# Loading group 0's second block of four k-tiles in two lots of two row tiles instead of one lot of four

## Chip, cores, metric

One core of one Trainium2 chip. The metric is device time in microseconds (us) of one execution of the program; a kernel's time is the median of its runs. The experiments ran on four chips, each with runs of the kernel before beside it.

## The reference

```python
def setup_inputs():
    m, k, n = 4096, 4096, 4096
    # a: (m, k), b: (k, n), bias: (n,), all float32, normal
def reference(a, b, bias):
    return np.tanh(np.matmul(a, b) + bias)
```

## The kernel before

8192 matmuls of 128x128 by 128x512 in f16. `a` and `b` are cast from f32 to f16 by the loading DMAs, which GpSimd issues. `a` also has to be turned: a load writes four quarters of 32 partitions (one DMA each), and VectorE transposes 32x32 blocks. The start-up treats eight row tiles of `a` specially: group 0 (`g0`, rows 0 to 3) and group 1 (`g1`, rows 4 to 7), with k in blocks.

```python
P, Q, QP = 128, 4, 32
G, KS, AN, BL, KM = 4, 8, 3, 4, 16

def load_a(m0, nmb, t0, nt):            # nmb x 32 rows, nt k-tiles
    an = anat.tile([P, nmb, nt * QP], fp16, name="an")      # anat: AN = 3 buffers
    for t, n in split(t0, nt):
        for q in (0, 2, 1, 3):
            ...
            nc.gpsimd.dma_start(out=an[ds(q * QP, QP), :, ...], in_=src...)
    return an

def pump():                             # loads in order, at most AN lots alive
    while queue and (queue[0][0] is None or live[0] < AN):
        ...

# order of the loads (cut)
want_a("g1b", G, 4 * P, G * Q, BL, BL)
for i in range(BL):
    want(load_b_next)                   # B tiles, k-tiles 4 to 7
want_a("g0b", G, 0, G * Q, BL, BL)      # "lot B": rows 0-3, k-tiles 4-7
want_a("g0c", G, 0, G * Q, KS, KM - KS) # "lot C": rows 0-3, k-tiles 8-15
for u in range(KS, KM, 2):
    want(lambda u=u: load_b_all(u, 2))  # B in four quarters, two k-tiles each

# TensorE and VectorE (cut)
for m in g0:
    turn(ats[m], "g0b", m * Q, BL, BL)  # transposes of lot B
down(ps, g1, KS - 1, KS, put_aside)
for m in g0:
    turn(ats[m], "g0c", m * Q, KS, KM - KS)
one_by_one(ps, g0, BL, KS, BL)          # 32 matmuls, need lot B
for m in g0:
    across(ps, (m,), KS, KS + 2, BL)    # k-tile 8 on: need lot C and B's quarters
across(ps, g0, KS + 2, KM - 1, BL)
```

The built program allows eight GpSimd DMAs in flight: in its list of waits, each waits for the landing of the one eight places before it. The traces agree: of the 1613 in the trace of before, none was issued before the one eight places earlier had landed, and 241 were issued less than 0.4 us after it.

Of the kernel before, what the change touches and what calls it, by code (L numbers as in the profile page):

```python
# [14 lines left out]
P = 128  # L15
Q = 4
# [7 lines left out]
def kernel(  # L24
# [18 lines left out]
    G = 4  # L43
    KS = 8
    AN = 3
    BL = 4
# [37 lines left out]
    def load_a(m0, nmb, t0, nt):  # L84
        an = anat.tile([P, nmb, nt * QP], fp16, name="an")
        for t, n in split(t0, nt):
            for q in (0, 2, 1, 3):
                k = t * P + q * BL * QP if t < KS else P * KS + (q * (KT - KS) + t - KS) * QP
                src = a[ds(m0, nmb * QP), ds(k, n * QP)]
                nc.gpsimd.dma_start(  # L90
                    out=an[ds(q * QP, QP), :, ds((t - t0) * QP, n * QP)],
                    in_=src.rearrange("(mb p) k -> p mb k", p=QP),
                )
        return an

    def transpose_a(at, an, mb0, t0, nt):

        for t, n in split(t0, nt):
            order = "P mb (k t) -> P mb t k" if t < KS else "P mb (t k) -> P mb t k"
            nc.vector.transpose(  # L100
                at[:, ds(t, n), :].rearrange("P t (mb p) -> P mb t p", p=QP),
                an[:, ds(mb0, Q), ds((t - t0) * QP, n * QP)].rearrange(order, k=QP),
            )
# [11 lines left out]
    def pump():  # L115
        while queue and (queue[0][0] is None or live[0] < AN):
            key, uses, load = queue.pop(0)
            made = load()
            if key is not None:
                live[0] += 1  # L120
                staged[key] = [made, uses]

    def want_a(key, uses, *where):
        queue.append((key, uses, lambda: load_a(*where)))

    def want(load):
        queue.append((None, 0, load))

    def turn(at, key, mb0, t0, nt):
        pump()  # L130
        transpose_a(at, staged[key][0], mb0, t0, nt)
        staged[key][1] -= 1
        if not staged[key][1]:
            live[0] -= 1
            pump()
# [6 lines left out]
    def finish(ps, addend, mi, c0, w=NB, o_sb=None, queues=(nc.sync,)):  # L142
# [22 lines left out]
    ats = [  # L165
        bpool.tile([P, KT, P], fp16, name=f"atx_{m}", tag=f"b_{4 + m}") for m in range(G)
    ] + [atp.tile([P, KT, P], fp16, name="at") for m in range(G)]
# [41 lines left out]
    def down(ps, ms, t0, t1, done):  # L209
        for m in ms:  # L210
            for j in range(J):
                for t in range(t0, t1):
                    mm(ps[m][j], ats[m], b_cur, t, j, False, t == t1 - 1)
                done(ps[m][j], m, j)
# [77 lines left out]
    want_a("g1b", G, 4 * P, G * Q, BL, BL)  # L292
    for i in range(BL):
        want(load_b_next)
    want_a("g0b", G, 0, G * Q, BL, BL)
    want_a("g0c", G, 0, G * Q, KS, KM - KS)
    for u in range(KS, KM, 2):
        want(lambda u=u: load_b_all(u, 2))
# [21 lines left out]
    one_by_one(ps, g1, 0, BL, 0)  # L320
    across(ps, g1, BL, KS - 1, 0)
    for m in g0:
        turn(ats[m], "g0b", m * Q, BL, BL)
    down(ps, g1, KS - 1, KS, put_aside)


# [127 lines left out]
```

## Time and profile before

| kernel before | us |
|---|---|
| median of 3 runs, before the change was made | 1781.98 (1781.78 to 1783.19) |
| median of 6 runs, with the runs beside the changed kernel | 1782.13 (1781.52 to 1783.19) |
| span of the profiled execution | 1780.6 |

The lines are shown in the prediction. They are read in this order: the page's busy row (TensorE works all the time), the chain that ended last in order of time (where the few stops are, and that none comes after 36.44 us), then stretches cut around the stops. Times in the traces count from the first instruction; "landing" is when a DMA's completion is signalled.

### The profile page before, as it was taken

The page shows a single profiled execution, that of the slowest core. Times are in us where ns is not written, and L with a number is a line of the kernel's source. Part 1 is how long each engine was busy: PE and PEld are TensorE (multiplying, and loading weights), DVE is VectorE, ACT ScalarE, POOL GpSimd, SP SyncE. Part 2 cuts the span into 40 slices and gives each one's busy share as a digit, 9 for nine tenths or more (in the row PEclk, how much of TensorE's full clock was granted, in tenths as well). Part 3 has the DMA queues.
Part 4 walks back from the last instruction along what each step waited for, and adds up shares of the span by engine and source line. Part 5 has one row for each costly group of instructions (what it writes and reads, how often), then busy time and mean ns, then how long its engine had stood idle before and what let it go on. Part 6 is the DMA issues. An engine that isn't in the chain of part 4 may idle for free.

```text
span 1780.6 us, 20859 instructions
## 1 busy us (share of the span) xinstructions
PE 1774.4 (100%) x8254; PEld 807.0 (45%) x8254; DVE 763.7 (43%) x682; ACT 172.9 (10%) x281; POOL 872.5 (49%) x1618
## 2 busy tenths in 40 slices
PE   9999999999999999999999999999999999999999
PEld 4444444444444444444444444444444444444444
DVE  3574443444334443444344443444344443444342
ACT  2021000000000000000000000000000000000001
POOL 7465566544565554444456554444544445444510
PEclk9999999999999999999999999999999999999999
DMA  9999999976999877767699997766777667766731
GB/s 183 205 193 177 173 162 166 141 125 110 166 176 164 145 112 116 118 116 120 113 168 173 159 149 116 119 115 109 129 116 121 107 108 121 119 114 109 117 77 42
DMA packets 281393, 238.94 MB, mean 134 GB/s; under 512 B 159056, under 2 KB 231760, under 8 KB 281296
## 3 DMA queue, kind: packets, MB, share of 16 engines
q0 software_dynamic: 243280, 167.88, 69.9%
q1 hardware_dynamic: 37728, 69.62, 11.0%
q8 instruction: 64, 1.05, 0.3%
q14 instruction: 33, 0.27, 0.0%
q10 hardware_dynamic: 288, 0.13, 0.0%
HBM read 337.64 MB, written 67.11 MB: 227 GB/s over the span
## 4 chain that ended last, share of the span: by engine, by line
PE 98%; DMA 1%; POOL 0%; issue 0%; DVE 0%; ACT 0%; POOLq 0%; DVEq 0%
PE ps L415 93%; PE ps L138 5%; DMA an<-in_a_dram 1%; DMA b<-in_b_dram 0%; POOL an L90 0%; POOL nat L246 0%; ACT o_sb L152 0%; DVE atx L100 0%; DVE o_sb L149 0%; POOL b L69 0%; POOL ident L264 0%; POOLq L264 0%; DVEq L149 0%; DVEq L100 0%; POOLq L438 0%
## 5 line engine op out<-in xcount | busy, mean ns | idle before, releaser
L415 PE MATMUL ps<-b,at 128*128 128x512 f16 x7712 | 1657.8, 378 | 0.0
L90 POOL DMA_DIRECT2D an<-in_a_dram x1492 | 805.9, 547 | 797.1 <-DVE at L100 558.6
L415 PEld LDWEIGHTS <-at 128*128 128x128 f16 x7712 | 754.6, 98 | 903.3
L100 DVE STREAM_TRANSPOSE at<-an 128x512 f16<-128x512 f16 (+1 forms) x380 | 565.5, 1539 | 78.2 <-DMA an<-in_a_dram 78.2
L149 DVE TENSOR_TENSOR o_sb<-ps,bias_bc 128x512 f32<-128x512 f32 (+1 forms) x243 | 165.6, 683 | 907.3 <-PE ps L415 697.7
L152 ACT ACTIVATE o_sb<-o_sb 128x512 f32<-128x512 f32 (+1 forms) x243 | 151.4, 624 | 1501.2 <-DVE o_sb L149 1501.2
L73 POOL DMA_DIRECT2D b<-in_b_dram x104 | 56.2, 544 | 14.1 <-DMA an<-in_a_dram 7.0
L138 PE MATMUL ps<-b,atx 128*128 128x512 f16 x256 | 56.2, 379 | 0.6 <-DVE atx L100 0.6
L138 PE MATMUL ps<-b,at 128*128 128x512 f16 x256 | 55.6, 379 | 0.0
L138 PEld LDWEIGHTS <-at 128*128 128x128 f16 x256 | 25.0, 98 | 30.2
L138 PEld LDWEIGHTS <-atx 128*128 128x128 f16 x256 | 24.8, 98 | 30.6 <-DVE atx L100 1.6
L100 DVE STREAM_TRANSPOSE atx<-an 128x512 f16<-128x512 f16 (+2 forms) x12 | 16.3, 1399 | 11.7 <-DMA an<-in_a_dram 11.7
L69 POOL DMA_DIRECT2D b<-in_b_dram x12 | 7.8, 654 | 22.4 <-PE ps L415 22.3
L152 ACT ACTIVATE spill<-spill 128x512 f32<-128x512 f32 x16 | 9.9, 630 | 84.4 <-DVE spill L149 84.4
L149 DVE TENSOR_TENSOR spill<-ps,spill 128x512 f32<-128x512 f32 x16 | 10.2, 674 | 6.2 <-PE ps L138 6.2
L181 DVE TENSOR_TENSOR spill<-spill,bias_bc 128x512 f32<-128x512 f32 x16 | 10.3, 681 | 3.5 <-DMA bias_bc<-in_bias_dram 3.5
L173 ACT COPY spill<-ps 128x512 f32<-128x512 f32 x16 | 8.0, 624 | 12.8 <-PE ps L138 12.8
L228 PE MATMUL ps<-zeros 128*128 128x512 f16 (+1 forms) x14 | 4.7, 504 | 1.3 <-DVE zeros L221 1.3
L176 DVE TENSOR_TENSOR spill<-ps,spill 128x512 f32<-128x512 f32 x8 | 4.8, 674 | 0.0
L228 PEld LDWEIGHTS <-zeros 128*128 128x128 f16 x14 | 1.6, 130 | 3.7 <-issue 2.5
L246 POOL DMA_DIRECT2D nat<-in_a_dram x4 | 2.3, 587 | 0.8 <-POOLq L438 0.8
L239 DVE CAST b<-spill 128x1024 f16<-128x1024 f32 x1 | 0.7, 694 | 4.3 <-DMA spill<-in_b_dram 4.3
(14 smaller groups left out, 9.1 us busy)
## 6 DMA issues: line engine op xcount, KB each, us to landing
an<-in_a_dram POOLq DMA_DIRECT2D x480, 192.0 KB, 5.1
out_dram<-o_sb SPq DMA_DIRECT2D x239, 256.0 KB, 2.7
an<-in_a_dram POOLq DMA_DIRECT2D x960, 32.0 KB, 2.7
b<-in_b_dram POOLq DMA_DIRECT2D x94, 256.0 KB, 8.1
b<-in_b_dram POOLq DMA_DIRECT2D x6, 1024.0 KB, 12.5
an<-in_a_dram POOLq DMA_DIRECT2D x32, 128.0 KB, 5.3
out_dram<-spill SPq DMA_DIRECT2D x16, 256.0 KB, 5.1
an<-in_a_dram POOLq DMA_DIRECT2D x12, 256.0 KB, 8.3
```

What stands on the lines that cost most here:

```text
L69: queue.dma_start(out=dst, in_=src[:, ds(t0 % BL, nt), :])
L73: nc.gpsimd.dma_start(out=bt[t0 // TB][ds(q * QP, QP), ds(t0 % TB, nt), :], in_=src.rearrange("(t p) n -> p t n", p=QP),)
L90: nc.gpsimd.dma_start(out=an[ds(q * QP, QP), :, ds((t - t0) * QP, n * QP)], in_=src.rearrange("(mb p) k -> p mb k", p=QP),)
L100: nc.vector.transpose(at[:, ds(t, n), :].rearrange("P t (mb p) -> P mb t p", p=QP), an[:, ds(mb0, Q), ds((t - t0) * QP, n * QP)].rearrange ...
L138: nc.tensor.matmul(ps, at[:, t, :], bt[t // TB][:, t % TB, ts(j, NB)], start=start, stop=stop)
L149: nc.vector.tensor_tensor(out=o_sb[:, piece], in0=ps[:, piece], in1=addend[:, piece], op=mybir.AluOpType.add)
L152: nc.scalar.activation(o_sb[:, piece], o_sb[:, piece], mybir.ActivationFunctionType.Tanh)
L173: nc.scalar.copy(aside(m, j), ps)
L176: nc.vector.tensor_tensor(out=aside(m, j), in0=ps, in1=aside(m, j), op=mybir.AluOpType.add)
L181: nc.vector.tensor_tensor(out=aside(m, j), in0=aside(m, j), in1=bias_bc[:, ts(j, NB)], op=mybir.AluOpType.add)
L228: nc.tensor.matmul(ps[:, ds(0, w)], zeros[:, :P], zeros[:, :w], start=i == 0, stop=i == n - 1)
L415: nc.tensor.matmul(ps, at[:, t, :], b_cur[t // TB][:, t % TB, ds(c0, w)], start=t == 0, stop=t == KT - 1,)
```

## The change

Intent: TensorE stops before the 32 matmuls that need lot B, and at first they need only row 0. With two lots the transposes of rows 0 and 1 can start when half of lot B has landed.

```diff
-    want_a("g0b", G, 0, G * Q, BL, BL)
+    want_a("g0b", 2, 0, 2 * Q, BL, BL)
+    want_a("g0b2", 2, 2 * P, 2 * Q, BL, BL)
     want_a("g0c", G, 0, G * Q, KS, KM - KS)
...
-        turn(ats[m], "g0b", m * Q, BL, BL)
+        turn(ats[m], "g0b2" if m > 1 else "g0b", m % 2 * Q, BL, BL)
```

## The prediction

> **What bounds the kernel now.** I read the page first: who is busy, the slices, the chain that ended last.
>
> ```profile
> span 1780.6 us, 20859 instructions
> PE 1774.4 (100%) x8254; PEld 807.0 (45%) x8254; DVE 763.7 (43%) x682; ACT 172.9 (10%) x281; POOL 872.5 (49%) x1618
> ...
> PE 98%; DMA 1%; POOL 0%; issue 0%; DVE 0%; ACT 0%; POOLq 0%; DVEq 0%
> ```
>
> TensorE is busy for 1774.4 of 1780.6 us; no transfer change can return more than the 6.2 us in which it is not. The chain in order of time says where those lie:
>
> ```profile
> 19.46 9.00 DMA an<-in_a_dram
> 28.46 0.03 DVEq L100
> 28.49 0.05 issue
> 28.54 0.72 DVE atx L100
> 29.26 0.05 issue
> 29.31 7.08 PE ps L138 x32
> 36.39 0.06 issue
> 36.44 83.04 PE ps L138 x384
> 119.48 1654.20 PE ps L415 x7680
> 1773.68 0.04 DVEq L149
> ```
>
> The piece issued at 19.46 and landing at 28.46 is the fourth DMA of the tile that the change splits (call it lot B: group 0's second block, four row tiles, four DMAs of 128 KB as f16). From 36.44 TensorE never stops again until its last matmul at 1773.68: 83.04 us for 384 matmuls is 0.216 us each, 1654.20 for 7680 is 0.215. So only the time at which TensorE begins at 36.44 matters, and whatever moves that moment moves the end one for one. Two stops lie just ahead of it. I cut the time into stretches around them:
>
> ```profile
> core 0: us, PE busy (x) PEld busy (x) DVE busy (x) ACT busy (x) POOL busy (x), PEclk, DMA share, GB/s
> 14.70:28.60 13.90, 13.90 (x66) 6.17 (x63) 3.30 (x7) 4.10 (x9) 8.65 (x15) 1.00 1.39 177
> 28.60:29.30 0.70, 0.15 (x1) 0.00 (x0) 0.70 (x2) 0.70 (x3) 0.54 (x1) 1.00 1.46 197
> 29.30:36.20 6.90, 6.89 (x32) 3.02 (x32) 4.00 (x5) 1.99 (x5) 3.42 (x7) 1.00 1.22 197
> 36.20:36.45 0.25, 0.20 (x2) 0.04 (x2) 0.25 (x2) 0.00 (x0) 0.25 (x1) 1.00 0.86 156
> ```
>
> Busy time counts a matmul's modelled 379 ns, so the stops look shorter than they are. By starts: matmuls should follow each other by 0.216, and the gaps between starts are 0.936 at 29.31 and 0.434 at 36.44. The first stop thus costs 0.72 us and the second 0.22, 0.94 in all. The first is lot B: its landing at 28.46 is followed by the first transpose at 28.54. For the second the waits name VectorE, but the first transpose of group 0's next lot (lot C, k-tiles 8 to 15) ran from 33.93 for 1.245 us and was over at 35.18. What ended at 36.35 was something else: the matmul of k-tile 8 also needs all four quarters of its B tile, and the fourth was issued at 28.74 and took 7.6 us to land:
>
> ```profile
> L73 POOL DMA_DIRECT2D b<-in_b_dram x1: 535/535/535, 28.7 to 28.7; - x1
> ...
> DMA to landing us min/median/max: 7.6/7.6/7.6
> ```
>
> So the releaser printed for the second stop (VectorE) is the later of two events by coincidence: a second transpose ended at 36.30 while the fourth quarter landed at 36.35. The bound of the start-up is the flow of the loads, of which lot B, lot C and those quarters are successive pieces. It runs full:
>
> ```profile
> DMA  9999999999999999999999999999999999999999
> GB/s 189 198 196 190 194 201 194 198 192 197 195 199 201 191 195 199 191 199 203 205 207 203 211 231 168 242 176 225 209 199 213 188 230 188 213 205 205 164 164 139
> ...
> b<-in_b_dram POOLq DMA_DIRECT2D x11, 128.0 KB, 6.2
> an<-in_a_dram POOLq DMA_DIRECT2D x1, 256.0 KB, 7.8
> ```
>
> That is the DMA view from 26 to 36 us: every slice at the top digit, about 197 GB/s of f16 written (twice that read, as the source is f32).
>
> **What the Trainium skill says.** "DMA: Bandwidth & Descriptors", section "Specifications", puts the fabric's ceiling at 435 GB/s. Here 256 KB of a quarter of B (f32) pass every 0.64 us, 411 GB/s, and 512 KB of lot C every 1.34 us, 391 GB/s: the trace agrees that there is little left. The same page, section "Anatomy of one DMA — SWDGE (gpsimd) path", gives about 2.0 us of fixed cost to each DMA. Here DMAs of `a` that were issued with nothing queued ahead landed 1.47 us at the earliest, 1.63 in the median, after their issue ended, payload included; somewhat less than the page's figure. "TensorE: Matmul & The Clock Gate", section "Wait — 56ns, not 53.3ns?", gives 215.7 ns from one 512-column matmul to the next; the trace has 215.4 to 216.3, so TensorE has no slack to recover a delay with.
>
> **The change part by part.** The instruction order of the two kernels differs in GpSimd's list alone, apart from renamings and which waits VectorE carries. Four DMAs of 32x16x128 become eight of 32x8x128, in the same place; bytes, row pieces (512 B of f32) and everything else stay. Matmuls: same.
>
> 1. The first half of lot B. Its four DMAs are issued when the four of lot B were: 16.54, 17.20, 17.85, 19.46 (each DMA waits for the landing of the one eight before, as the program's waits show, and those eight are unchanged). Lot B's DMAs landed at 26.22, 26.95, 27.71 and 28.46, 0.75 apart, behind the B tiles ending at 25.75. Halves should take 0.37 each: last one at about 25.75 + 4 x 0.37 = 27.2. Transposes of rows 0 and 1 take 0.6 each: done by 28.5, the first by 27.9. TensorE comes free at 29.31 - 0.72 = 28.59. Stop one disappears: 0.72 us.
> 2. The second half. Its four DMAs take the places in the row of eight that lot C had, so they are issued at 21.2, 22.2, 25.1 and 26.0, and land by 28.5, or by 26.0 + 0.6 + 1.5 to 2.0 = 28.1 to 28.6 for the last if the fixed cost sets it. Row 2 is needed 16 matmuls after 28.59, at 32.05. More than 2 us of slack, so no wait.
> 3. Lot C. It now comes four places later: each DMA waits for a half of lot B (25.9 to 27.2 landed), GpSimd is free only at 26.6, and it needs 0.65 for each: issues at 26.6, 27.3, 27.9 and 28.6, not 21.2 to 26.0. Its buffer is also another, that of group 1's second block, released when its transposes ended at 21.74: long past, no wait. The flow before it holds until about 28.5 (landing), and lot C's first can land no sooner than 27.26 + 1.5 + about 1.2 of payload = 29.96, against 29.78 before. So a hole of about 0.2 us, from nothing to 0.8 if the fixed cost is the page's 2.0.
> 4. The four quarters of B behind lot C: issued at about 29.2 to 30.9, ahead of their turn in the flow; the last lands at 36.35 plus the hole. TensorE's 32 matmuls now run from 28.59 to 35.51 and it then waits for 36.35 + 0.09 = 36.44 plus the hole. Stop two grows from 0.22 to 0.94.
> 5. GpSimd issues four DMAs more, 4 x 0.58 = 2.3 us, of which about 0.4 is won back by shorter ones. It had that much idle time between 20 and 26.
>
> Sum: -0.72 + 0.72 + hole = 0 to 0.8, most likely about 0.2 us.
>
> **Rivals.** First, a real gain: if the second stop were VectorE's (as the waits print it) or the flow had slack, TensorE would start k-tile 8 earlier, up to 0.72 us, and the end would be at 1781.3. Against it: the fourth quarter's landing at 28.74 + 7.6, and the full slices. Second, a loss: eight DMAs in flight hold fewer bytes when some are halves, and the issue of lot C falls 5.4 us later for its first DMA. If the queues run dry near 28 for longer than I think, lot C, the quarters and all of TensorE's remaining work shift by 1 to 1.5 us: 1783.0 to 1783.5. For it: with the second half's last DMA issued at 26.0, only 2 us of work are left ahead of lot C. Against it: the landings are set by the engine that lags most, and it still has its backlog then. Third, a lasting loss, as the three `a` buffers turn by one more place from here: the tile after next always takes the buffer of three loads earlier, which holds after the change as before, and the later loads wait for the DMA eight before them as they did. I see no route by which it reaches the steady part, with its 1654 us of uninterrupted matmuls.
>
> **Range and chances.** 1781.98 + 0.2 gives 1782.2. The mechanism spans -0.7 to +1.5; the three runs of before spread over 1.4 us (1781.78 to 1783.19). Together: 1781.1 to 1783.7. Two per cent is 35.6 us, six times all of TensorE's idle time on one side, and on the other more than the whole start-up up to its first long run of matmuls (29.3 us) would have to be lost again. So 0.99 for within 2%.
>
> **What would show it.** In the profile of after: no gap in TensorE between 14.8 and 35.5; one gap there of about 0.9 us, ended by B's quarter; first transpose of group 0's second block at about 27.2 and the third at about 28.6; lot C issued from 26.6; the 384 matmuls from 36.4 to 36.7, the 7680 from 119.5 to 119.7. Wrong would be: a start of that run before 36.2 (then the flow was not the bound), after 37.3 (then the hole was larger), or any stop of TensorE after it.

## The result

The changed kernel: median 1783.43 us of 6 runs (1782.84 to 1785.50), the kernel before 1782.13 of 6. The ratio is 1.0009, 95% interval 0.9996 to 1.0022; a ratio here is the mean time of one kernel's runs over that of the other's of the same rounds, so not quite the ratio of the medians. It is the same within 2%. The median lies 1.3 us above before, where 0.2 had been predicted, still inside the predicted range; the mean of the six runs, 1783.81, lies just above it. One run, the profiled one, took 1785.50.

The chain of the changed kernel, in order of time (start, length, what; a further line in the source moves the last matmuls from L415 to L416):

```profile
25.65 2.54 POOL an L90 x4
28.19 1.56 POOL b L73 x3
29.75 8.11 DMA b<-in_b_dram
37.87 0.14 issue
38.00 84.63 PE ps L138 x384
122.64 1654.20 PE ps L416 x7680
```

There is no TensorE piece before 38.00 on this chain: the run of matmuls begins when a quarter of B lands at 37.87. The 384 matmuls take 84.63 us, not 83.04. The stretches say why (columns as in the prediction; PEclk is the granted TensorE clock):

```profile
14.70:35.40 20.70, 20.70 (x98) 9.27 (x95) 6.14 (x11) 6.77 (x14) 12.79 (x24) 1.00 1.28 164
35.40:38.00 2.60, 0.24 (x2) 0.03 (x1) 2.60 (x3) 0.00 (x0) 2.10 (x4) 0.97 1.06 187
38.00:41.30 3.30, 3.30 (x8) 1.16 (x9) 1.79 (x2) 0.00 (x0) 2.66 (x5) 0.51 1.11 196
```

No stop until 35.4, as predicted. Then one stop instead of two, of 2.53 us (2.745 from start to start, less 0.216). TensorE's clock is at half from 37.84 to 41.26 by the trace's clock records (a stretch's PEclk is their mean): the next eight matmuls start 0.38 to 0.43 us apart, most of them 0.427. That loses a further 1.6 us.

The timeline of the changed kernel, some lines (start, length, instructions, in brackets the idle time before and what ended it):

```profile
26.29 1.30 DVE L100 STREAM_TRANSPOSE atx<-an 128x512 f16<-128x512 f16 x2 [4.94 <-DMA an<-in_a_dram]
...
28.57 7.07 PE L138 MATMUL ps<-b,atx 128*128 128x512 f16 x32
...
38.00 3.48 PE L138 MATMUL ps<-b,atx 128*128 128x512 f16 x8 [2.37 <-DMA b<-in_b_dram]
```

The first transposes of lot B come at 26.29 instead of 28.54, and the 32 matmuls at 28.57 instead of 29.31. The change does what it is for. The time is lost in the loads. The DMA view of the changed kernel from 24 to 34 us, 40 slices:

```profile
DMA  9999999979999789999999999999999999999999
GB/s 173 165 175 176 154 150 169 117 73 93 133 105 69 34 72 100 125 143 170 172 178 203 195 201 193 166 164 170 180 199 193 188 182 186 191 193 223 191 223 213
```

The fourteenth slice (27.25 to 27.5) moved 34 GB/s, and full flow is back only after 29. Before, the flow was at 190 to 200 there. The DMA at fault is lot C's first; from its tile's view (issued 25.65, 0.642 us of issue):

```profile
L90 POOL DMA_DIRECT2D an<-in_a_dram x1: 642/642/642, 25.6 to 25.6; - x1
...
DMA to landing us min/median/max: 4.7/4.7/4.7
```

From the end of issue at 26.29 to landing at 30.37 it took 4.08 us. The prediction had put 1.5 + about 1.2 = 2.7 there.

A second trace of each kernel was taken among the experiments. The four side by side, all from the traces (us from the span's start):

| | before | before, again | changed | changed, again |
|---|---|---|---|---|
| lot B's last DMA lands | 28.46 | 28.12 | 27.72 | 28.08 |
| lot C's first: issued | 21.20 | 21.48 | 25.65 | 25.99 |
| lot C's first: end of issue to landing | 7.93 | 7.31 | 4.08 | 4.02 |
| lot C's first: landing after lot B's last | 1.32 | 1.31 | 2.65 | 2.57 |
| last quarter of B for k-tile 8 lands | 36.35 | 36.01 | 37.87 | 37.26 |
| k-tile 8 starts | 36.44 | 36.10 | 38.00 | 37.40 |
| idle before the 32 matmuls | 0.72 | 0.30 | 0 | 0 |
| idle before k-tile 8 | 0.22 | 0.22 | 2.53 | 1.86 |
| lost to half clock | 0 | 0 | 1.6 | 0 |
| span | 1780.6 | 1780.3 | 1783.7 | 1781.6 |

The spans are accounted for. First pair: 38.00 - 36.44 = 1.56, plus 1.6 for the clock, is 3.2; the spans differ by 3.1. Second pair: 37.40 - 36.10 = 1.30; the spans differ by 1.3.

The second pair is the plain case: the hole before lot C (2.57 instead of 1.31) makes all of the delay. Its chain:

```profile
30.09 7.17 DMA b<-in_b_dram
37.26 0.14 issue
37.40 83.04 PE ps L138 x384
```

In the first pair there is more. The hole (2.65 instead of 1.32) was partly made up, since lot B had landed 0.74 us sooner than before; but lot C's third DMA landed 2.06 us after its second, instead of 1.34, and B's four quarters took 0.23 us longer in all. Without these, TensorE's stop would have been about 1.6 us. Two other traces with halves show such a second gap (1.75 us before lot C's third DMA in the kernel with the fill, 1.10 before a quarter of B in the kernel with one buffer), the other two don't; its cause isn't known.

### The profile page after: what moved, and what is told of

Read it like the earlier page. It is cut to its first block, busy times and chain, and to the rows that moved or that the text cites. A ratio compares the mean times of both kernels' runs of the same rounds, so it can differ in the third digit from the quotient of the medians.

```text
span 1783.7 us, 20866 instructions
## 1 busy us (share of the span) xinstructions
PE 1776.4 (100%) x8254; PEld 806.3 (45%) x8254; DVE 764.2 (43%) x682; ACT 173.0 (10%) x281; POOL 871.2 (49%) x1622
## 4 chain that ended last, share of the span: by engine, by line
PE 97%; DMA 1%; POOL 1%; issue 0%; ACT 0%; DVE 0%; POOLq 0%; DVEq 0%
PE ps L416 93%; PE ps L138 5%; DMA b<-in_b_dram 1%; POOL an L90 0%; POOL nat L246 0%; POOL b L69 0%; POOL b L73 0%; ACT o_sb L152 0%; DVE o_sb L149 0%; POOL ident L264 0%; POOLq L264 0%; DVEq L149 0%; POOLq L439 0%
## 5 line engine op out<-in xcount | busy, mean ns | idle before, releaser
L416 PE MATMUL ps<-b,at 128*128 128x512 f16 x7712 | 1657.8, 378 | 0.0
L416 PEld LDWEIGHTS <-at 128*128 128x128 f16 x7712 | 753.1, 98 | 904.7
```

The lines of the kernel that those rows point to most:

```text
L416: nc.tensor.matmul(ps, at[:, t, :], b_cur[t // TB][:, t % TB, ds(c0, w)], start=t == 0, stop=t == KT - 1,)
```

## The experiments

My theory after the result had two parts. (1) The halves push lot C's issue behind the eight halves, to 25.7; its first DMA needs 4 us from there, so the flow breaks and everything behind it comes later. (2) The two stops become one, which is sometimes long enough for the clock to drop. Rivals: an unlucky execution; the turn of the buffers (lot C now takes another one); too few bytes in flight rather than the late issue; a clock drop that has nothing to do with the stop.

### The changed kernel again

Edit: none.

> The changed kernel once more, unaltered, for a second trace and more times. In its first trace two stops of TensorE became one: the matmul of k-tile 8 started at 38.00 instead of 36.44, and the first 8 matmuls after it came at 0.427 us instead of 0.216. Theory 1 (a hole in the loads, plus a drop of TensorE's clock where the stop gets long): the start of k-tile 8 again after 36.9, with lot C's first landing 2 us or more after the last of lot B; half clock after the stop only if the stop is near 2.5 us. The ratio to before is 1.0003 to 1.0012. Theory 2 (a single unlucky execution, no systematic cost): start at 36.3 to 36.7 and a ratio within 0.0002 of 1.

Median 1783.18 (5 runs, 1782.76 to 1785.92), before 1782.12 (9 runs), ratio 1.0009 (0.9995 to 1.0023). The hole is there again (2.57 us between landings, table above), so the loss is systematic. The profiled execution had no clock drop after 1.86 us of idle time; one other of the five, 1785.92, shows a mean clock of 0.999. In all, 2 of the 11 runs of the changed kernel show 0.999. The two traces of before that stand beside them in the table come from different calls. The 26 runs of before whose clocks were listed beside the experiments all show 1.000.

### Lot B in one buffer, by eight halves

```diff
-    want_a("g0b", G, 0, G * Q, BL, BL)
+    queue.append(("g0b", G, lambda: load_a_parts(0, G * Q, BL, BL, 2)))  # one tile; rows 0-1, then rows 2-3
```

> The kernel before with lot B kept as one tile in one buffer, but loaded by eight half DMAs in the changed kernel's order; the transposes of rows 0 and 1 wait for the first four alone. Buffers turn as in the kernel before. If the cost comes from the smaller DMAs (eight in flight hold half the bytes, lot C is issued later), this is the changed kernel again: lot C's first issue near 25.7, a hole of over 1 us in the landings before lot C, start of k-tile 8 after 36.9, ratio to the kernel before 1.0003 to 1.0012. If it comes from the turn of the buffers (lot C waiting for another buffer), this is as fast as the kernel before, 36.4 and a ratio of 1.0000.

Median 1784.02 (1783.16 to 1786.31), ratio 1.0013 (1.0001 to 1.0026). Lot C's first was issued at 26.12 and landed 4.14 us after the end of issue, 2.73 after lot B's last; k-tile 8 started at 38.10 after 2.62 us of idle time, and the clock dropped here too, at 38.52 (2 of the 5 runs show 0.999). From the stretches of this kernel:

```profile
35.40:38.10 2.70, 0.24 (x2) 0.03 (x1) 2.70 (x3) 0.00 (x0) 1.92 (x4) 1.00 1.06 178
38.10:41.90 3.80, 3.80 (x10) 1.40 (x11) 1.54 (x2) 0.00 (x0) 2.90 (x7) 0.55 1.13 203
```

The buffers turn as before, and the loss is there. So it is the splitting into more DMAs, not the buffers.

### Lot B by sixteen quarters

Edit: as the last, with 4 in place of 2 (one row tile a part).

> The kernel before with lot B in one buffer, loaded in sixteen quarter DMAs (one row tile each) instead of four. In all five traces with eight halves, lot C's first DMA landed 4.0 to 4.1 us after its own issue had ended, whatever was queued ahead, and its issue waits for the landing of the DMA eight places before. Theory 1 (late issue plus that fixed 4.0 us): lot C's first is issued at about 30, lands at about 35, k-tile 8 starts at 41 to 43, TensorE's stop of 5 us or more also halves its clock for 8 matmuls: 1787 to 1791 us, ratio to before 1.003 to 1.005. Theory 2 (a hole of fixed length whenever the queue restarts, not tied to the issue): 1783 to 1784.5, as with eight.

Median 1789.54 of 4 runs (1788.92 to 1790.32), before 1781.84, ratio 1.0043 (1.0028 to 1.0058): inside what theory 1 expected, far from theory 2. Lot C's first was issued at 29.96 and took 4.8 us from there:

```profile
L102 POOL DMA_DIRECT2D an<-in_a_dram x1: 652/652/652, 30.0 to 30.0; - x1
...
DMA to landing us min/median/max: 4.8/4.8/4.8
```

It landed at 34.75, 4.13 us after the end of issue, though lot B's last had landed 3.1 us earlier. k-tile 8 started at 41.59. Against before that is 5.15 us later, plus 1.7 at half clock, 6.9 together; the spans are 1787.5 and 1780.6. The clock dropped at 38.28, while TensorE was still idle; the stretches:

```profile
35.40:38.10 2.70, 0.28 (x2) 0.00 (x0) 0.00 (x0) 0.00 (x0) 0.97 (x3) 1.00 1.42 199
38.10:41.60 3.50, 0.01 (x1) 0.04 (x2) 2.60 (x3) 0.00 (x0) 2.38 (x5) 0.53 1.12 204
41.60:45.20 3.60, 3.60 (x9) 1.27 (x10) 2.02 (x2) 0.00 (x0) 2.71 (x7) 0.51 1.12 195
```

So the loss follows lot C's issue, which follows the number of small DMAs ahead of it. In this trace the eight places aren't the only reason: from 25.16 on GpSimd issued one quarter after the other without a pause, 0.53 us each, so the last nine of them took 4.8 us of its own time.

### Two quarters of B between the halves

```diff
+    want(lambda: load_b_q(KS, 2, (0, 2)))
     want_a("g0b2", 2, 2 * P, 2 * Q, BL, BL)
     want_a("g0c", G, 0, G * Q, KS, KM - KS)
-    for u in range(KS, KM, 2):
+    want(lambda: load_b_q(KS, 2, (1, 3)))
+    for u in range(KS + 2, KM, 2):
```

> The changed kernel with two of the four quarters of B's k-tiles 8 and 9 moved in between the two halves of lot B. As many DMAs, as many halves, the same GpSimd work; but when lot C is issued, larger DMAs are in flight (512 KB of f32 more, about 1.3 us of flow). If the hole is a queue that runs dry for want of bytes in flight, it closes: lot C's four land 1.3 to 1.4 us apart from the DMA ahead of them on, its last at about 35.0, and k-tile 8 starts at 36.3 to 36.8; ratio to the changed kernel 0.9985 to 0.9997, about that of the kernel before. If GpSimd's issuing or the buffers make the hole, it stays, and k-tile 8 starts at 37.5 to 38.5, later than in the changed kernel by the transposes that now follow the flow more closely.

Median 1783.91 (1783.53 to 1784.83), ratio 1.0011 (0.9999 to 1.0024). My expectation failed; k-tile 8 started between the two times that I had named. The larger DMAs in flight did not close the hole: lot C's first was issued later still, at 27.16, and landed 3.97 us after the end of issue. The last half landed 0.96 after the one before (0.37 in a full flow) and lot C's first 1.74 after that (1.34 in a full flow), an excess of 1.0 us. k-tile 8 began at 37.34, and three short stops of 0.13 to 0.25 followed, as the transposes now end close to their use. So more bytes in flight alone don't close it. That the wait counts from lot C's own issue is argued from the 4.0 us, which stayed the same; as this edit also moved the issue by 1.5 us, it doesn't separate the two.

### Matmuls of zeros in the stop

```diff
+    for _ in range(7):
+        nc.tensor.matmul(ps[G - 1][J - 1], zeros[:, :P], zeros, start=False, stop=False)
     for m in g0:
         across(ps, (m,), KS, KS + 2, BL)
```

> The changed kernel with 7 matmuls of zeros added into a running accumulation in the place where TensorE stops (7 x 0.216 = 1.5 us, result unchanged). If the half clock after the stop comes from the length of the idle time, the matmuls of k-tile 8 come at 0.216 from the first, at a granted clock of 1.00, although they start as late as in the changed kernel (36.9 to 38.0); the slow executions vanish (none above 1784.2) and the ratio to the changed kernel is 0.9990 to 0.9999. If the drop has another cause (a periodic or power event), it stays in some executions, and the times are those of the changed kernel.

Median 1783.99 (1783.37 to 1784.87), ratio to before 1.0011 (0.9998 to 1.0024). TensorE's timeline, changed kernel with the fill:

```profile
35.46 1.67 PE L333 MATMUL ps<-zeros 128*128 128x512 f16 x7
37.78 4.48 PE L138 MATMUL ps<-b,atx 128*128 128x512 f16 x20 [0.65 <-DMA b<-in_b_dram]
```

No run of five showed a clock of 0.999 and none reached 1785 (one, 1784.87, lies above the 1784.2 that I had named), but the time did not fall: it is 0.8 us above the changed kernel's median of the same rounds. In the trace k-tile 8 started at 37.78, 0.38 later than in the second trace of the changed kernel, since the quarter landed later (37.64), and there is a stop of 0.19 us at 51.8. Whether the fill itself delays the loads is open. As a remedy it is worth nothing here; with a drop in only 2 of 11 runs of the changed kernel, its absence in 5 proves little either.

### TensorE's stop made longer, loads untouched

Edit to the kernel before, the order of lot C's transposes:

```diff
-    for m in g0:
+    for m in (1, 2, 0, 3):
         turn(ats[m], "g0c", m * Q, KS, KM - KS)
```

> The kernel before, loads unchanged; only the order of four transposes of lot C on VectorE is changed (row tiles 1, 2, 0, 3 instead of 0, 1, 2, 3), so that TensorE's second stop gets longer by a known amount: row 0 is ready at 37.4 and k-tile 8 starts at about 37.5, after 1.3 us of idle time. Theory (the end moves one for one, no clock drop at this length): +1.1 us, ratio 1.0005 to 1.0008, matmuls at 0.216 us after the stop, no run with a clock of 0.999. If the time is made in the loads and not by TensorE's start at k-tile 8, no change.

Median 1783.23 of 4 runs (1782.39 to 1783.52), before 1781.84, ratio 1.0008 (0.9991 to 1.0024): +1.4 by the medians, where 1.1 was expected. The profiled execution was its fastest; the loads had come about 1 us early in it (lot B's last at 27.47), and TensorE still waited for row 0 until 36.50, 0.99 us of idle time, with the clock at 1.00. Against the traces of before that start isn't late (36.44 and 36.10), nor is the span longer (1780.7), so the trace doesn't show the loss of the other three runs. All four runs show 1.000.

The second edit puts row 0 last and once more:

```diff
+    for m in (1, 2, 3, 0):
+        if m == 0:
+            transpose_a(ats[0], staged["g0c"][0], 0, KS, KM - KS)
         turn(ats[m], "g0c", m * Q, KS, KM - KS)
```

> As e_stop1, with row 0 transposed last and once more than needed: k-tile 8 starts at about 39.7, after 3.5 us of idle time. Theory (an idle time of 2.5 us or more halves the clock for the first 3.4 us or so after it, without any change to the loads): +3.3 us of waiting and +1.7 us of 8 matmuls at 0.427 instead of 0.216, together +4.5 to +5.5 us, ratio 1.0025 to 1.0031, in every run a clock of 0.999. If the half clock comes from the loads or by chance: +3.3 us, ratio 1.0018 or 1.0019, 0.216 us from the first matmul.

Median 1786.81 of 4 runs (1785.49 to 1787.35), +5.0 us, ratio 1.0026 (1.0011 to 1.0041). k-tile 8 started at 39.49 after 3.67 us of idle time; the stretches:

```profile
35.80:39.40 3.60, 0.19 (x1) 0.00 (x0) 3.57 (x4) 0.00 (x0) 3.00 (x6) 1.00 1.08 170
39.40:43.50 4.10, 4.01 (x11) 1.49 (x12) 0.03 (x1) 0.00 (x0) 3.20 (x6) 0.59 1.16 193
```

Half clock with the loads as before: the drop comes from the idle time. It is not certain, though: three runs show 0.999, the fourth, 1785.49, shows 1.000.

The clock records of the traces say more. In all fifteen, the time between two changes of the clock is a whole number of times 3.413 us (3.41, 6.83, 30.72, 34.13, ..., 1774.93), and the moment of the first rise lies between 4.15 and 7.23, differently in each. So the clock changes only at the ends of windows of 3.413 us, whose position differs from one execution to the next. Counted window by window from the first rise on, TensorE's idle time tells drops from none in every case:

| kernel | its stop (us) | idle in one window | clock at that window's end |
|---|---|---|---|
| changed | 2.53 | 2.37 | half, at 37.84 |
| one buffer, eight halves | 2.62 | 2.62 | half, at 38.52 |
| sixteen quarters | 6.07 | 2.76, then 3.31 | half, at 38.28 |
| row 0 last and once more | 3.67 | 0.88, then 2.79 | half, at 40.12 |
| changed, again | 1.86 | 0.78, then 1.08 | full |
| two quarters of B between | 1.73 | 1.73 | full |

The windows at the programs' ends, after the last matmuls, agree: 2.04 us and less left the clock full, 2.39 us and more halved it. So it isn't the stop's length alone but how much of it falls into one window: the limit lies between 2.04 and 2.37 us. The same stop can keep the clock when a window's end divides it; that this is what happened in the fourth run isn't shown, as it wasn't traced.

### What one DMA takes in quiet

Loads that nobody reads, after the kernel's last load (before, otherwise unaltered; correct result).

```diff
+    probe(0, 16)                    # lot C's form, alone
+    for q in (0, 2, 1, 3):
+        probe(q, 16)                # four at once
+    probe_half(3)                   # lot B's half, alone
+    for q in (3, 0, 2, 1):
+        probe_half(q)
+    probe(1, 8)
+    probe(1, 16)                    # lot C's form, alone
```

> The kernel before with twelve loads more, which nobody reads, after its last load, where the queue is empty: one DMA of lot C's form alone; four of it at once; one half of lot B's form alone; four at once; one of 32x8x256; one of lot C's form. Measures from the end of issue to landing. If lot C's 4.0 us belong to its form (start and payload of one DMA with 512 rows of 1 KB), the single ones take 3.8 to 4.2 and the half 2.4 to 2.9. If they come from the company (descriptors of the next DMAs written while the first starts, engines that lag), single ones take 2.6 to 3.0 and halves 1.7 to 2.0, and the first of four takes longer than the single one. The time of the kernel stays that of before, within 0.001.

1782.05 us, one run. The first single DMA of lot C's form:

```profile
L429 POOL DMA_DIRECT2D an<-in_a_dram x1: 652/652/652, 1713.3 to 1713.3; - x1
...
DMA to landing us min/median/max: 3.7/3.7/3.7
```

From the end of issue: 3.08 and 3.21 us for the two single ones, 3.17 for the first of four. That is between my two expectations. The half alone took 2.61, the first of four halves 2.59, as expected if the time belongs to the form. The second single one ran beside a transpose on VectorE (1737.3 to 1740.6), so a transpose at its side is hardly what costs 0.9 us in the start-up. So of the 1.35 us by which 2.7 was too small, some 0.5 belong to the form, and about 0.9 to something in the start-up. Two further runs were to find that.

Edit of the first: before, with four B tiles, eight halves and four of lot C, then four B tiles, four whole ones of lot B and four of lot C.

> The kernel before with two further sets of loads in the quiet end, read by nobody: first the changed kernel's order (four B tiles of 512 KB, eight halves of lot B, four of lot C), then that of before (four B tiles, four whole ones, four of lot C). A single DMA of lot C's form took 3.1 to 3.2 us from the end of its issue to landing in e_probe, 4.0 to 4.1 in the start-up. If the extra 0.9 us come from the DMAs queued ahead (engines that lag), lot C's first takes 3.9 us or more in the first set too, and a hole of over 1 us stands before it. If they come from something else in the start-up, it takes 3.1 to 3.4 and the hole is 0.4 us or less. In the second set there is no hole either way (1.3 to 1.5 us from landing to landing).

1781.91 us, one run; void for its question. The buffers' own waits pulled the first set apart: lot C's first was issued at 1740.78, 6.4 us after the last half had landed. It took 3.59 us, beside a store of the output. In the second set there was no hole before lot C: its first landed 1.32 us after lot B's last.

Edit of the second: set X, lot C's four and B's four quarters into an empty queue; set Y, sixteen quarters of lot B ahead of the same eight; buffers free beforehand.

> The kernel before with two sets of loads in its quiet end, read by nobody. Set X: lot C's four DMAs into an empty queue, B's four quarters right behind them. Set Y: sixteen quarters of lot B, then the same eight, which is the order of e_onetile16. From the end of issue to landing, lot C's first took 4.14 us in e_onetile16's start-up and 3.1 to 3.6 in the quiet end. If the DMAs written behind it make the difference, both X and Y take 3.9 us or more; if those queued ahead do, Y alone; if neither, both take 3.1 to 3.6 and the difference belongs to the start-up's conditions.

1784.62 us, one run (its late loads held up the last output stores, and both kernels were slower: before took 1782.83). Set Y's first of lot C:

```profile
L436 POOL DMA_DIRECT2D an<-in_a_dram x1: 654/654/654, 1767.4 to 1767.4; - x1
...
DMA to landing us min/median/max: 3.9/3.9/3.9
```

3.27 us from the end of issue, in the same order of DMAs in which the start-up took 4.13. Set X took 4.55, but an output store was in flight beside it from 1744.16 to 1748.64, so it says nothing. The order of the DMAs around it therefore doesn't explain the 0.9 us, as far as one run shows; what in the start-up does, stays open.

### The second trace of before

Edit: none.

> The kernel before, unaltered, for a second trace of it. Theory: two short stops of TensorE again (before the 32 matmuls and before k-tile 8), 0.9 us in all give or take 0.4, k-tile 8 started at 36.1 to 36.8, lot C's four landings 1.30 to 1.40 us apart from lot B's last on (no hole), no half clock. If one trace of before was luck, k-tile 8 starts after 36.9 or lot C shows a hole.

1781.97 us, one run. Two short stops, 0.30 and 0.22 us; lot C's four landed 1.31 to 1.36 apart from lot B's last on; no hole, no half clock. It is the second column of the table.

### Two versions that should have been better

The split made in lot C instead, lot B whole:

```diff
-    want_a("g0c", G, 0, G * Q, KS, KM - KS)
-    for u in range(KS, KM, 2):
+    want_a("g0c", 2, 0, 2 * Q, KS, KM - KS)
+    want(lambda: load_b_all(KS, 2))
+    want_a("g0c2", 2, 2 * P, 2 * Q, KS, KM - KS)
+    for u in range(KS + 2, KM, 2):
```

> The kernel before with the split made in lot C instead (rows 0 and 1, then B's quarters for k-tiles 8 and 9, then rows 2 and 3), lot B whole. Lot C's first half keeps its early issue (21 to 26). By the theory (issue well ahead, so no hole; only half of lot C ahead of the quarters) the quarters land at about 34, the second stop is gone (0 to 0.1 us), the first stays at 0.5 to 0.8: k-tile 8 starts at 36.1 to 36.3, 0.2 us gained, ratio 0.9997 to 1.0001. If splitting a lot costs by itself, over 1 us is lost, as in the changed kernel.

Median 1782.07 of 5 runs, before 1781.79 of 9, ratio 1.0001 (0.9988 to 1.0015). What was expected of the loads came: the quarters landed by 33.47, k-tile 8 started without a stop, and the split opened no hole; the first half of lot C kept its early issue (22.08). The time was given back later. The chain:

```profile
29.04 9.67 PE ps L138 x44
38.71 0.02 issue
38.73 10.98 PE ps L138 x50
49.71 0.03 issue
49.74 0.02 DVEq L176
49.76 0.10 issue
49.86 0.66 DVE spill L176
50.52 0.04 issue
50.57 69.23 PE ps L138 x320
```

0.18 us are lost at row 2, and 0.60 at 50.57. There TensorE waits for an accumulator that VectorE empties only after transposing group 1's next lot, which landed at 47.44 here against 46.38 in the second trace of before. A slack that the traces of before hide became the next stop.

Both splits, with the quarters of B between the halves of lot B (changed kernel):

```diff
+    want(lambda: load_b_all(KS, 2))
     want_a("g0b2", 2, 2 * P, 2 * Q, BL, BL)
-    want_a("g0c", G, 0, G * Q, KS, KM - KS)
-    for u in range(KS, KM, 2):
+    want_a("g0c", 2, 0, 2 * Q, KS, KM - KS)
+    want_a("g0c2", 2, 2 * P, 2 * Q, KS, KM - KS)
+    for u in range(KS + 2, KM, 2):
```

> The changed kernel's early half of lot B, but with B's four quarters for k-tiles 8 and 9 between the halves and lot C split by rows as well, so that what TensorE needs comes in the order in which it needs it, and the late issue of the later lots is not waited for. By the theory: no first stop; the quarters land at about 29.6, lot B's second half at 30 to 31.2, lot C's first half at about 34; k-tile 8 starts at 35.5 to 35.8; small stops of 0 to 0.5 us at rows 2 and 3. 0.4 to 0.8 us better than before, ratio 0.9995 to 0.9999. If the theory of the fixed time from issue to landing is wrong, a stop of over 1 us stays before k-tile 8 or row 2 and the time is that of the changed kernel.

Median 1784.23 of 5 runs (1783.48 to 1784.71), ratio 1.0014 (1.0001 to 1.0026). It failed. Lot C's first half-size DMA was issued at 27.92 and landed 4.26 us after the end of issue, though in quiet that form took 2.31; it landed 1.86 us after lot B's last instead of the 0.67 of a full flow. Stops of 0.76, 0.25, 0.67, 0.25 and 0.53 us follow, 2.5 in all. So a late issue cost as much for 256 KB of f32 here as for 512 KB elsewhere (4.0 to 4.1). That the time isn't a fixed part plus a payload is not shown by it: lot B's second half was still landing until 30.90, 2.4 us after the end of this issue (1.4 us in the changed kernel), so more of the 4.26 us was spent behind it.

## Why the prediction was right or wrong

**Right.** Step 1 (the early half ends the first stop): the 32 matmuls began at 28.57, predicted 28.59 (the first transpose came at 26.29, 0.9 us sooner than predicted, which gained nothing). Step 2 (the second half costs nothing). Step 4 (the stop is carried over to k-tile 8, and the quarters of B end it, not VectorE): the trace after names the DMA of B. The bound, the flow of the loads, and the one-for-one passage of a delay to the end (plus what the clock costs): both pairs of spans. The rival of a real gain fell, as argued. The buffers are not the cause, as step 3 said; the kernel with one buffer shows it.

**Wrong.** Step 3, the term "27.26 + 1.5 + about 1.2 of payload". The issue came sooner than assumed (25.65 and 25.99, not 26.6), but the time from its end to landing was 4.08 and 4.02 us, not 2.7. I took the 1.5 from the smallest DMAs of `a` in the steady part and added a payload. In quiet, lot C's form takes 3.1 to 3.3; in the start-up, issued late, 4.0 to 4.1 in six traces. The flow ahead also ended sooner than "about 28.5", at 27.72 and 28.08. The hole was therefore 1.3 and 1.2 us between landings in the two traces, not 0.2; the issue, 1.0 and 0.6 us sooner than assumed, kept it from being longer, which was luck. The range named for it, up to 0.8, was too narrow as well. The prediction's own sign of a larger hole, a start after 37.3, came: 38.00 and 37.40. My second rival, "the queues run dry near 28 for longer than I think", is what happened; the argument against it, that the engine that lags most still has its backlog, did not hold: the last half landed at 27.72, and at 27.25 to 27.5 the flow was down to 34 GB/s.

**Missing.** Step 4 turned two stops of 0.72 and 0.22 us into one and added them, as if a stop cost only its length. A stop of 2.5 us can also cost 1.6 us at half clock. The Trainium skill says so ("TensorE: Matmul & The Clock Gate", section "What's actually happening"): the clock falls to half after an idle window of about 3.4 us, and the windows run freely. I had read that page for the spacing of matmuls alone. The traces agree on the half clock, on the windows (3.41 us, at a position that differs from run to run), and so on chance: 2 of 11 runs of the changed kernel, 3 of 4 after 3.7 us. They differ on how much idle time it takes (last section).

**Two comparisons with the skill that the prediction read wrongly.** The 411 and 391 GB/s count bytes of f32 that are read; about 197 GB/s of f16 were written into the core's memory (SBUF), and the 435 GB/s of "DMA: Bandwidth & Descriptors", section "Specifications", are the ceiling on that side. So they don't show that little is left; that the flow was full rests on the slices and on the even landings (0.64 and 1.34 us apart). And the 1.47 and 1.63 us count from the end of issue, while the page's 2.0 us include the issue's own work: from the start of issue the same loads took 2.0 us at the earliest and 2.2 in the median, so they are not less than the page's figure.

**Left open.** Why a load issued late in the start-up needs 0.9 us more than in quiet. Whether the fill delays loads. Where the second gap of the first trace comes from. And each ratio of the changed kernel to before has an interval that includes 1; that the loss is real rests on the traces, on two sets of rounds that agree, and on the kernels with lot B in eight halves or sixteen quarters, whose intervals lie above 1.

## What to carry to other kernels

Splitting a load to get its first part sooner uses up places among the DMAs in flight and time of the engine that issues them: look at which load behind it is now issued later, and take its time from issue to landing from a trace of the same phase, not from a quiet one. Where a flow of loads is the bound, an earlier start of one consumer only moves the wait to the next. And two short stops of TensorE are cheaper than one of the same length once the long one can put over 2 us into one window of the clock (the limit lay between 2.04 and 2.37 us here).

## What the Trainium skill lacked or had wrong

- "TensorE: Matmul & The Clock Gate", section "What's actually happening": ties the drop to an idle window of about 3.4 us. Here a window of 3.41 us need not be idle throughout: 2.37 us of idle time in one were enough, 2.04 were not. And a stop of 3.67 us was not always enough (one of four runs kept 1.000).
- "DMA: Bandwidth & Descriptors", section "Anatomy of one DMA — SWDGE (gpsimd) path": 2.0 us plus bytes at 436 GB/s gives estimates of 2.15 us for 64 KB and 3.2 us for 512 KB of f32. Counted from the start of issue, the first fits (2.0 us at the earliest and 2.2 in the median, loads of `a` with nothing ahead in the trace of before), and the second is too short: 3.7 and 3.8 in quiet. It has no figure for a load that is issued late in a busy start-up: 4.6 to 4.8 us for 512 KB, 4.0 to 4.1 of them after the issue's end.
- The same page has nothing on how many DMAs a program keeps in flight. Here eight, each waiting for the one eight before, which is this program's own; with eight and sixteen small DMAs ahead, the next large one was issued 4.5 and 8.8 us later than before.
